# How far apart the rows of one load lie: 48 adjacent rows per partition in place of groups of 8

## The chip, the cores and the metric

The kernel runs on one core of a Trainium2 chip. The metric is device time in microseconds (us), lower is better. "The Trainium skill" names the notes on the chip; its pages are cited by title. A packet is one contiguous piece of a transfer, carried by one of the core's 16 DMA engines; a transfer has landed when its completion is counted. Packet durations, counts and start times, where given, are from the packet records of the trace; everything else is from views of the profile, of which the main lines are shown.

## The reference

```python
x = np.random.randn(8192, 8192).astype(np.float32)      # 256 MiB
return np.linalg.norm(x, ord=np.inf, axis=1)            # max |x| of each row, 8192 results
```

The input is read once, and one number is kept per row of 32 KiB. So this is a stream of loads with a reduction behind it.

## The kernel before

Each partition takes 64 rows: 48 in the bulk, fetched by 24 loads of 8 MiB (two adjacent rows, 64 KiB, per partition), and 16 in a tail, whose pieces get smaller towards the end so that little work is left after the last byte. Three buffers hold tiles. VectorE reduces. SP (SyncE) issues the loads, ACT (ScalarE) issues two of the three outputs.

```python
TAIL = [[8192]]*8 + [[4096,4096]]*5 + [[2048]*4]*2 + [[2048,2048,2048,1024,512,512]]

G = 4; B = 2; BUFS = 3                       # defaults of the function
n_bulk_rows = rows // P - n_tail             # 48
A = n_bulk_rows // (G * B)                   # 6
split = n_bulk_rows * P
x_b   = x[:split].rearrange("(a p n b) c -> a n p (b c)", p=P, a=A, n=G, b=B)
out_b = out[:split].rearrange("(a p n b) -> p a (n b)", p=P, a=A, n=G, b=B)
x_t   = x[split:].rearrange("(p t b) c -> t p (b c)", p=P, b=B)      # tail, pitch 512 KiB
...
for a in range(A):
    for n in range(G):
        t = sbuf.tile([P, B * cols + 16], F32, tag="t")
        nc.sync.dma_start(out=t[:, : B * cols], in_=x_b[a, n])
        absmax(r_bulk[:, a, n * B : (n + 1) * B], t[...])
nc.scalar.dma_start(out=out_b, in_=r_bulk[:])
for i in range(0, n_tail, B):                # the tail, smaller and smaller pieces
    ...
        nc.sync.dma_start(out=t[:, at : at + w], in_=x_t[i // B][:, at : at + w])
        ...
```

With G = 4, a partition holds 8 adjacent rows of each of 6 blocks. Seen from one load, the 128 pieces lie 8 x 32 KiB = 256 KiB apart; this distance is the pitch. The output of the bulk has, per partition, 6 runs of 8 numbers: 768 runs of 32 B.

## Time and profile before

| | before |
|---|---|
| time, median | 629.97 us (3 runs, 629.9 to 630.3) |
| bytes read | 268.44 MB, 427 GB/s over the span |
| one bulk load | 19.34 us, from one reduction's start to the next |
| one bulk reduction | 17.22 us |

Lines from the page of the profile: bytes moved in 40 slices of the span; the group of the bulk reductions (busy us, mean ns, then idle time before them and its cause); and two groups of DMA issues with the time from issue to landing.

```profile
span 628.1 us, 196 instructions
GB/s 401 413 455 413 455 413 455 413 455 413 455 413 455 409 459 413 455 413 455 413 455 413 455 413 455 413 455 413 455 405 430 434 435 432 420 432 432 424 426 274
...
L63 DVE TENSOR_REDUCE r_bulk<-t 128x2 f32<-128x16384 f32 x24 | 413.3, 17219 | 70.5 <-DMA t<-in_x_dram 70.5
...
t<-in_x_dram SPq DMA_DIRECT2D x24, 40.7
out_dram<-r_bulk ACTq DMA_DIRECT2D x1, 24.0 KB, 57.9
```

The reductions need 413 us and wait 70.5 us, always for loads; a load of 8,388,608 B in 19.34 us is 433.7 GB/s. The load stream is the bound. Longer windows (columns: stretch, its length, busy time of VectorE and GpSimd, clock, DMA share, GB/s):

```profile
42.00:484.00 442.00, 395.34 (x23) 0.00 (x0) 1.00 1.00 433
484.00:519.00 35.00, 35.00 (x6) 0.00 (x0) 1.00 1.01 432
519.00:560.00 41.00, 40.62 (x7) 0.00 (x0) 1.00 1.00 429
560.00:604.00 44.00, 43.06 (x12) 0.00 (x0) 1.00 1.00 426
```

First SP's waits (in total, times, longest), then the same wait in the chain that ended last (start us, us, what):

```profile
SPq L82 <- DMA out_dram<-r_bulk: 23.2, 1, 23.2
```

```profile
519.10 0.33 SPq L82
519.43 23.23 another core or an unknown queue
542.67 0.33 SPq L82
```

A tail load is not issued until the bulk's output has landed. The program says why: the DMAs use eight completion counters in turn, and the load eight places after the output needs the output's counter (in the trace both name counter 102). No data is involved.

### The profile page before, as it was taken

To read this page: it belongs to the slowest core of one execution; us is meant where nothing else is said; L and a number is where in the kernel's file an instruction comes from. 1 tells how busy PE (TensorE), PEld (TensorE's weight loads), DVE (VectorE), ACT (ScalarE), POOL (GpSimd) and SP (SyncE) were. 2 spreads that over 40 slices of the span, in tenths; PEclk is the share of its full clock that TensorE was granted. 3 is DMA by queue.
4 is the path that set the end of the run, shared out by engine and by line. 5 is a ranking of instruction groups with operands and counts; after the bars stand their busy time and mean duration, and the time that the engine had idled before them with its cause. 6 is when DMAs were issued, how large, how long until landed. Compare 5 with 4: busy or idle time off the path is not lost.

```text
span 628.1 us, 196 instructions
## 1 busy us (share of the span) xinstructions
DVE 552.7 (88%) x58; POOL 0.2 (0%) x4
## 2 busy tenths in 40 slices
DVE  0588988889988889888898888998889999999998
POOL 0000000000000000000000000000000000000000
DMA  9999999999999999999999999999999999999996
GB/s 401 413 455 413 455 413 455 413 455 413 455 413 455 409 459 413 455 413 455 413 455 413 455 413 455 413 455 413 455 405 430 434 435 432 420 432 432 424 426 274
DMA packets 9138, 268.49 MB, mean 427 GB/s; under 512 B 1968, under 2 KB 1968, under 8 KB 2352
## 3 DMA queue, kind: packets, MB, share of 16 engines
q1 hardware_dynamic: 8208, 268.44, 99.1%
q10 hardware_dynamic: 928, 0.03, 0.1%
q14 instruction: 2, 0.02, 0.0%
HBM read 268.44 MB, written 0.03 MB: 427 GB/s over the span
## 4 chain that ended last, share of the span: by engine, by line
DMA 64%; DVE 30%; another core or an unknown queue 4%; issue 1%; SPq 0%
DMA t<-in_x_dram 64%; DVE r_bulk L63 23%; DVE part L63 5%; DVE t L63 1%; SPq L82 0%; DVE r_fin L63 0%; SPq L68 0%
## 5 line engine op out<-in xcount | busy, mean ns | idle before, releaser
L63 DVE TENSOR_REDUCE r_bulk<-t 128x2 f32<-128x16384 f32 x24 | 413.3, 17219 | 70.5 <-DMA t<-in_x_dram 70.5
L63 DVE TENSOR_REDUCE part<-t 128x1 f32<-128x4096 f32 (+2 forms) x26 | 130.0, 5067 | 1.3 <-DMA t<-in_x_dram 1.3
L63 DVE TENSOR_REDUCE t<-t 128x1 f32<-128x2048 f32 (+2 forms) x5 | 8.6, 1746 | 0.4 <-DMA t<-in_x_dram 0.4
L60 DVE MEMSET part<- 128x60 f32 x1 | 0.1, 108 | 0.8 <-PEq L114 0.8
L63 DVE TENSOR_REDUCE r_fin<-t 128x1 f32<-128x517 f32 x1 | 0.7, 692 | 0.0
L63 DVE TENSOR_REDUCE r_tail<-part 128x15 f32<-128x60 f32 x1 | 0.2, 216 | 0.0
L114 POOL MEMSET const-bfloat16-1.0<- 128x1 bf16 x1 | 0.1, 101 | 0.0
L114 POOL MEMSET const-uint8-127<- 128x1 uint8 x1 | 0.1, 101 | 0.0
L114 POOL MEMSET const-float32-0.0<- 128x1 f32 x1 | 0.1, 98 | 0.2 <-issue 0.2
L114 POOL MEMSET const-float32-1.0<- 128x1 f32 x1 | 0.1, 98 | 0.0
## 6 DMA issues: line engine op xcount, KB each, us to landing
t<-in_x_dram SPq DMA_DIRECT2D x8, 4096.0 KB, 37.0
t<-in_x_dram SPq DMA_DIRECT2D x10, 2048.0 KB, 30.4
t<-in_x_dram SPq DMA_DIRECT2D x11, 1024.0 KB, 24.6
t<-in_x_dram SPq DMA_DIRECT2D x1, 512.0 KB, 15.9
t<-in_x_dram SPq DMA_DIRECT2D x2, 256.0 KB, 13.2
t<-in_x_dram SPq DMA_DIRECT2D x24, 40.7
out_dram<-r_bulk ACTq DMA_DIRECT2D x1, 24.0 KB, 57.9
out_dram<-r_tail ACTq DMA_DIRECT2D x1, 7.5 KB, 5.6
```

The costliest lines, as they stand in the source:

```text
L60: nc.vector.memset(part[:], 0.0)
L63: nc.vector.reduce_max(out=o, in_=i, axis=X, apply_absolute_value=True)
L114: nc = _bacc.Bacc("TRN2", target_bir_lowering=False, num_devices=1)
```

## The change

The intent is a simpler layout: one block, in which a partition holds all its 48 bulk rows side by side, and writes its results as one run of 192 B.

```diff
-    G: int = 4,
+    G: int = 24,
```

A becomes 1. Pieces of one load now lie 48 x 32 KiB = 1.5 MiB apart, and one load touches addresses over 192 MiB in place of 32 MiB. The output of the bulk becomes 128 runs of 192 B. The instructions on the other engines, the sizes and the order of loads are the same.

## The prediction

> **What bounds the kernel now.** The load stream. The table of windows gives 433 GB/s at a DMA share of 1.00 from 42 to 484 us, nearly all of the bulk. One 8 MiB bulk load arrives each 19.34 us (starts of the reductions in the timeline): 433.7 GB/s. The Trainium skill, "DMA: Bandwidth & Descriptors", section Specifications, puts the fabric ceiling at 435 GB/s; the trace agrees, so nothing is left to win in the bulk. VectorE needs 17.22 us per tile and waits about 2.1 us each time; it follows the loads.
>
> **What the change does.** The 24 loads of 128 pieces of 64 KiB stay, in the same order and size; so do the reductions, buffers and tail. Two things change.
>
> 1. Pieces of one load lie 1.5 MiB apart in place of 256 KiB. The skill (same page, Latency and other measured facts, "HBM row pitch at large powers of two") reports copies that lose rate at pitches of 2 MiB (164 GB/s) and 4 MiB (103), with 207 at 512 KiB and 214 when padded, and only infers aliasing. 1.5 MiB is three times 512 KiB: modulo 2, 4, 8 or 16 MiB its pieces fall on the same set of places as those of pitch 512 KiB. The tail of this very kernel has pitch 512 KiB, and there the windows give 432 GB/s (484 to 519 us, and 560 to 574). So I expect no loss: 19.3 us per bulk load as before. If the pitch cost 1% of rate, that would be 4.6 us over the bulk.
>
> 2. The bulk's output is 128 runs of 192 B in place of 768 of 32 B. Now it takes 57.9 us from issue to landing: 48 small packets on each of 16 engines, each apparently taking its turn behind a 32 KiB load packet (estimate: 4 MiB at 433 GB/s is 9.7 us for 8 packets per engine, 1.21 us each; 48 x 1.21 = 58). With 8 per engine it should land in about 10 us. The waits show the SP queue held for 23.2 us by that output, from 519.4 to 542.7 us in the chain, before the next tail loads. This wait should vanish. It is worth little: meanwhile the queue still had loads to run (426 GB/s from 519 to 545 us), and only 543 to 546 us shows a dip, to 371 GB/s: (1 - 371/433) x 3 us = 0.4 us. The page gives that whole queue 0.1% of the DMA time, so the saved packets add at most 0.5 us.
>
> **On the critical path:** 0 for the pitch, -0.3 to -0.8 us for the output.
>
> **Predicted time:** 629.5 us, 80% range 628.4 to 631.2. Chances: faster by over 2%: 0.01; within 2%: 0.95; slower by over 2%: 0.04.
>
> **What would show it.** Right: reductions of the bulk start 19.3 us apart, VectorE idle before them about 70 us again, 433 GB/s in the bulk windows; the bulk's output lands in about 10 us; the 23 us wait is gone from SP's waits and the chain; no dip after 543 us. Wrong on the pitch: bulk loads further apart, GB/s lower at a DMA share still 1.00, VectorE idle longer. Wrong on the output: it still takes over 30 us, or the wait stays, or the wait goes and the total gains over 1 us.
>
> **What would make it wrong.** HBM treating 1.5 MiB worse than the tail's 512 KiB (one load now spans 192 MiB, not 32); earlier tail loads meeting the reductions so that buffers come free at a worse time; the wait on SP resting on something other than that output.

## The result, and the profile after

| | before | after |
|---|---|---|
| time, median of 6 runs each | 630.14 us (629.90 to 630.55) | 630.34 us (629.88 to 630.69) |
| ratio of after to before | | 1.0003, 95% interval 0.9990 to 1.0015 |
| bulk's output, issue to landing | 57.9 us | 14.3 us |
| SP's wait on it | 23.2 us | none |

Ratios here and below are the mean time of one kernel's runs over that of the other's of the same rounds, so not quite the ratio of the medians quoted.

The time is the same. The page, the windows, and the chain where the wait was:

```profile
span 628.6 us, 196 instructions
...
L63 DVE TENSOR_REDUCE r_bulk<-t 128x2 f32<-128x16384 f32 x24 | 413.3, 17220 | 71.0 <-DMA t<-in_x_dram 71.0
...
t<-in_x_dram SPq DMA_DIRECT2D x24, 40.7
out_dram<-r_bulk ACTq DMA_DIRECT2D x1, 24.0 KB, 14.3
```

```profile
42.00:484.00 442.00, 394.87 (x23) 0.00 (x0) 1.00 1.00 433
484.00:519.00 35.00, 35.00 (x5) 0.00 (x0) 1.00 1.00 430
519.00:560.00 41.00, 40.66 (x7) 0.00 (x0) 1.00 1.00 430
560.00:604.00 44.00, 42.97 (x12) 0.00 (x0) 1.00 1.01 427
```

```profile
485.10 51.65 DVE part L63 x6
536.75 0.02 issue
536.77 0.33 SPq L82
```

The wait of 23 us is gone from the chain, and the stretch in which it sat (519 to 560 us) moves 430 GB/s in place of 429. The tail did not get shorter: from the first tail reduction to the end of the span it is 628.1 - 484.62 = 143.5 us before and 628.6 - 485.10 = 143.5 us after.

### The profile page after: what moved, and what is told of

Its sections match the earlier page's. It is cut to its first block, busy times and chain, and to the rows that moved or that the text cites. A ratio compares the mean times of both kernels' runs of the same rounds, so it can differ in the third digit from the quotient of the medians.

```text
span 628.6 us, 196 instructions
## 1 busy us (share of the span) xinstructions
DVE 552.7 (88%) x58; POOL 0.2 (0%) x4
## 4 chain that ended last, share of the span: by engine, by line
DMA 65%; DVE 32%; issue 1%; another core or an unknown queue 0%; SPq 0%
DMA t<-in_x_dram 65%; DVE r_bulk L63 23%; DVE part L63 8%; DVE t L63 1%; DVE r_fin L63 0%; SPq L68 0%; SPq L82 0%
## 6 DMA issues: line engine op xcount, KB each, us to landing
out_dram<-r_bulk ACTq DMA_DIRECT2D x1, 24.0 KB, 14.3
```

## The experiments

Four questions: is the output's form worth anything? Was the 23 us wait hidden, and by how much? Does the pitch matter at all on this chip, and if so, is it distance or a power of two? And does the length of a piece matter? Ten kernels were run. The first call (e1 to e4) ran on one chip, the other two on another; before took the same time on both, to 0.3 us. Seven of the ten put results in wrong places, so that one thing changes at a time; in each of those the loads, reductions and sizes are those of a right kernel.

| run | pitch of the bulk | tail | bulk's output | median us | ratio to before (95%) |
|---|---|---|---|---|---|
| before | 256 KiB | 512 KiB | 32 B runs | 630.04 to 630.33 | 1 |
| after | 1.5 MiB | 512 KiB | 192 B | 630.34 | 1.0003 (0.9990 to 1.0015) |
| e1 | 256 KiB | 512 KiB | 192 B | 629.86 | 0.9997 (0.9984 to 1.0010) |
| e2 | 1.5 MiB | 512 KiB | 32 B | 630.38 | 1.0007 (0.9995 to 1.0019) |
| e3 | 256 KiB | 512 KiB | 8 B | 638.23 | 1.0130 (1.0117 to 1.0143) |
| e5 | 64 KiB | 512 KiB | 192 B | 630.39 | 0.9998 (0.9984 to 1.0012) |
| e10 | 512 KiB | 512 KiB | 192 B | 630.70 | 1.0008 (0.9996 to 1.0021) |
| e9 | 1 MiB | 1 MiB | 192 B | 641.35 | 1.0183 (1.0163 to 1.0203) |
| e8 | 1.94 MiB | 1.94 MiB | 192 B | 629.97 | 0.9995 (0.9983 to 1.0008) |
| e4 | 2 MiB | 2 MiB | 192 B | 662.68 | 1.0524 (1.0496 to 1.0552) |
| e6 | 1.5 MiB, 16 KiB pieces | 512 KiB | 192 B | 634.31 | 1.0066 (1.0049 to 1.0083) |
| e7 | 2 MiB, 16 KiB pieces | 2 MiB | 192 B | 724.14 | 1.1493 (1.1438 to 1.1549) |

### e1 and e2: one half of the change at a time

e1 keeps the loads of before and takes the output's form of after; e2 does the reverse.

```diff
 e1, from before
-    out_b = out[:split].rearrange("(a p n b) -> p a (n b)", p=P, a=A, n=G, b=B)
+    out_b = out[:split].rearrange("(p k) -> p k", p=P)
-    nc.scalar.dma_start(out=out_b, in_=r_bulk[:])
+    nc.scalar.dma_start(out=out_b, in_=r_bulk[:].rearrange("p a k -> p (a k)"))
 e2, from after
-    out_b = out[:split].rearrange("(a p n b) -> p a (n b)", p=P, a=A, n=G, b=B)
+    out_b = out[:split].rearrange("(s p k) -> p s k", p=P, s=6)
-    nc.scalar.dma_start(out=out_b, in_=r_bulk[:])
+    nc.scalar.dma_start(out=out_b, in_=r_bulk[:].rearrange("p a (s k) -> p (a s) k", s=6))
```

> Loads as before (256 KiB apart), output as after (128 runs of 192 B, so results land in wrong places on purpose). Theory H (the wait was hidden: the DMA engines had loads queued through all of it, so the output's form is worth nothing): within 0.3 us of before, about 630.1, with the output landing in about 14 us and SP's wait on it gone. Rival C (cancellation: the output's form gains 0.3 to 0.8 us and the wider pitch loses as much): 629.3 to 629.8, ratio 0.9987 to 0.9995. If the pitch makes the start of the stream late, the third bulk reduction starts at 61.5 us here as in before; if that was chance, anywhere from 61.4 to 62.0.

> Loads as after (1.5 MiB apart), output in 768 runs of 32 B as before (results in wrong places on purpose). Theory H: about 630.2, within 0.3 us of after, although the output takes about 58 us again and holds SP for about 23 us. Rival C: 630.5 to 631.1. If the pitch makes the start late, the third bulk reduction starts at about 61.9 us as in after.

e1 took 629.86 us and e2 630.38 us. The waits followed the output's form and not the pitch: SP's wait on the output is gone in e1, and in e2 it is there again at 23.1 us:

```profile
SPq L84 <- DMA out_dram<-r_bulk: 23.1, 1, 23.1
```

And yet e2 is within 0.1 us of after (630.34, from another call). So adding the 23 us wait back costs nothing that shows (theory H). The large cancellation of theory C is not there either: e1 is 0.2 us below before, less than C asked for, and the interval of its ratio spans 1. A pitch effect of some 0.4 us, from the start of the stream, is hinted at: the third bulk reduction starts at 61.47 us before and 61.34 in e1, at 61.93 in after and 61.67 in e2. It is taken up again with e5 and e10.

### e3: a longer wait

How much longer could the output take before it costs time? e3 splits it into 3072 runs of 8 B.

```diff
 e3, from before
-    out_b = out[:split].rearrange("(a p n b) -> p a (n b)", p=P, a=A, n=G, b=B)
+    out_b = out[:split].rearrange("(s p k) -> p s k", p=P, k=2)
-    nc.scalar.dma_start(out=out_b, in_=r_bulk[:])
+    nc.scalar.dma_start(out=out_b, in_=r_bulk[:].rearrange("p a (s k) -> p (a s) k", k=2))
```

> As before, but the output in 3072 runs of 8 B, 192 per DMA engine (wrong places on purpose), to lengthen the wait on SP. One packet per 1.21 us load packet would make it 232 us. Theory S (the wait limits itself: once the loads already issued, 226 MiB, have run dry at about 548 us, the small packets no longer queue behind loads and finish at once): the wait ends near 549 to 552 us, DMA idles 2 to 4 us, total 632 to 635. Rival L (each small packet keeps its turn time whatever else is queued): SP held until about 717 us, total over 790. If the wait had no margin at all in before, the form of the dose does not matter and the total stays within 0.5 us.

It took 638.23 us, 8.2 us more than before. The wait did limit itself, as theory S said: SP was held 35.4 us and not 200. From the table of windows and the chain of e3:

```profile
545.00:549.00 4.00, 3.45 (x2) 0.00 (x0) 1.00 1.01 426
549.00:552.00 3.00, 3.00 (x1) 0.00 (x0) 1.00 0.52 28
552.00:555.00 3.00, 3.00 (x2) 0.00 (x0) 1.00 0.00 0
555.00:557.00 2.00, 2.00 (x1) 0.00 (x0) 1.00 0.53 106
557.00:558.00 1.00, 1.00 (x1) 0.00 (x0) 1.00 0.84 344
```

```profile
519.63 35.39 another core or an unknown queue
555.02 0.02 issue
555.03 0.33 SPq L84
```

The loads that had been issued ran dry at about 549 us. Of the 3072 small packets 946 had been through at 549.0 us, at the pace of about one per load packet; the other 2126 were through at 551.1 us. The size was off: expected 2 to 4 us of idle DMA and 632 to 635 us in total, measured 6.7 us and 638.23. The 6.7 us run from the start of the last load packet (549.4 us) to the start of the next (556.0 us): 1.7 us for the remaining packets, 3.9 us in which no packet moves until SP sees the output landed (555.0 us), and 1 us to the first new bytes; then the stream needs until 558 us to fill up. Expectation S had left out the landing and the fill.

This also gives an estimate of the margin in before: its SP was free at 542.7 us, and in e3 the loads already issued lasted to about 549 us, so the wait was hidden with some 6 us to spare.

### e4: a pitch of 2 MiB

The whole matrix in one layout, 64 adjacent rows per partition, with a correct result.

```diff
 e4, from after
-    x_b = x[:split].rearrange("(a p n b) c -> a n p (b c)", p=P, a=A, n=G, b=B)
-    x_t = x[split:].rearrange("(p t b) c -> t p (b c)", p=P, b=B)
+    x_p = x.rearrange("(p r b) c -> r p (b c)", p=P, b=B)
 (loads from x_p[a * G + n] and x_p[A * G + i // B]; outputs likewise)
```

> As after, but the whole matrix in one layout: 64 adjacent rows per partition, bulk and tail both at a row pitch of 2 MiB, a power of two; correct result. Theory P0 (with one core loading, the DMA engines bound each packet at 2.42 us per 64 KiB and the pitch does not show): 630.2, bulk reductions 19.34 us apart. Rival P2 (a power-of-two pitch loses rate, in the proportion 164 to 214 that the skill's page gives for copies at 2 MiB): 25 us per bulk load, total about 820. The tail here has pieces of 16 KiB and less at 2 MiB: P2 would show at least there, as packets of 16 KiB over 0.61 us.

It took 662.68 us, 5.2% more than before. P0 is refuted: the pitch shows. P2's total of about 820 us is refuted as well; only its weaker form holds, that packets of 16 KiB take over 0.61 us (0.64 on average here). The profile is of the slowest of the six runs (666.14 us). The windows of e4:

```profile
0.00:60.00 60.00, 28.00 (x3) 0.20 (x4) 1.00 0.97 367
60.00:120.00 60.00, 50.52 (x4) 0.00 (x0) 1.00 1.01 428
200.00:460.00 260.00, 229.69 (x14) 0.00 (x0) 1.00 1.00 432
480.00:520.00 40.00, 40.00 (x4) 0.00 (x0) 1.00 1.01 410
600.00:640.00 40.00, 28.35 (x10) 0.00 (x0) 1.00 1.01 313
```

In all of these stretches the DMA engines are busy; they only move less. The first three reductions start at 26.8, 49.3 and 71.3 us (22.8, 42.1 and 61.5 before); from 200 us on the loads come at full rate from the same kind of addresses; and the tail, whose pieces get shorter, is slow again, down to 313 GB/s. Packets of 8 KiB took 0.49 us on average in place of 0.31. Of the 36.3 us that this profile is longer than that of before, the bulk lost 12.5 (its last reduction starts at 480.00 us, not 467.49), 9.8 of them by the third load; the tail lost the other 23.8. So most of the 5.2% is not from the 64 KiB pieces of the bulk but from the shorter ones of the tail.

### e8 and e9: distance, or a power of two?

1.5 MiB was free and 2 MiB cost 33 us, so either distance matters and 1.5 MiB was just near enough, or the power of two does. e8 goes almost as far as 2 MiB with an odd multiple of 64 KiB; e9 comes nearer, with a power of two.

```diff
 e8, from after (62 adjacent rows; the last pair per partition from the 256 rows left over)
+    x_p = x[: 62 * P].rearrange("(p r b) c -> r p (b c)", p=P, b=B)
+    x_e = x[62 * P :].rearrange("(p b) c -> p (b c)", b=B)
 e9, from after (two blocks of 32 adjacent rows)
+    x_p = x.rearrange("(a p r b) c -> a r p (b c)", a=2, p=P, b=B)
```

> As the 2 MiB run, but 62 adjacent rows per partition: row pitch 1.94 MiB (31 x 64 KiB), and the last pair of rows of each partition taken from the 256 rows left over (results in wrong places on purpose). Theory A (power-of-two alignment: engines that read the same place modulo a large power of two slow one another; distance itself costs nothing): 629.7 to 630.5, like before, and reductions 19.3 us apart from the first. Rival D (distance, or the span of addresses that one load touches: 0 at 256 KiB, about 0.4 us at 1.5 MiB, 32 us at 2 MiB): over 650, with the first four loads 20 to 27 us apart as in the 2 MiB run.

> Row pitch 1 MiB in bulk and tail (two blocks of 32 rows per partition; wrong places on purpose). Theory A: between 512 KiB or 1.5 MiB (under 0.5 us) and 2 MiB (32 us), so 633 to 645, with the loss in the first loads and in the tail. Rival D: like after or less, 629.9 to 630.4, since 1 MiB is less than 1.5 MiB. The two differ in sign against after: A slower by over 2 us, D not slower.

Windows of e8, then of e9:

```profile
0.00:60.00 60.00, 34.55 (x3) 0.20 (x4) 1.00 0.98 419
60.00:120.00 60.00, 52.37 (x4) 0.00 (x0) 1.00 1.01 437
```

```profile
0.00:60.00 60.00, 28.99 (x3) 0.20 (x4) 1.00 0.98 375
60.00:120.00 60.00, 50.80 (x4) 0.00 (x0) 1.00 0.99 426
200.00:460.00 260.00, 228.99 (x14) 0.00 (x0) 1.00 1.00 430
480.00:640.00 160.00, 156.32 (x34) 0.00 (x0) 1.00 0.96 411
```

The tail of before, to compare with the last line of e9:

```profile
468.00:628.00 160.00, 156.00 (x34) 0.00 (x0) 1.00 0.97 414
```

The nearer pitch is the slower one: 1 MiB costs 11.0 us (641.35 against 630.33), 1.94 MiB costs nothing (629.97). Distance, and the span of addresses, is out: of the pitches tried, the two powers of two from 1 MiB up cost time, and no other does. These two are also the only multiples of 1 MiB; whether 3 MiB, say, would cost too was not tried. One part of the expectation for e9 missed: its tail lost nothing. From the last bulk reduction's start to the end of the span it took 160.5 us (479.79 to 640.3), as before (467.49 to 628.1: 160.6). All of its loss, 12.3 us in the profile, is in the bulk, which thus lost as much at 1 MiB as at 2 MiB (12.5); what sets e4's 33 us apart is its tail.

### e10 and e5: 512 KiB and 64 KiB

```diff
-    G: int = 4,
+    G: int = 8,      (e10; e5 has G = 1; both with the 192 B output of e1)
```

> Bulk at 512 KiB (groups of 16 rows), tail unchanged at 512 KiB, output in 192 B runs (wrong places on purpose). The prediction's argument was that 1.5 MiB, three times 512 KiB, meets the same places modulo powers of two as 512 KiB. If so: as after, 630.2 to 630.5, with the third bulk reduction at about 61.7 to 61.9 us. If the 0.4 us of after come from distance: as with 256 KiB, 629.8 to 630.0, third reduction at about 61.4.

> Bulk pitch 64 KiB, so that each load is one contiguous 8 MiB block; output in 192 B runs (wrong places on purpose). Theory A with its floor at the DMA engines' own rate: 629.6 to 630.0, no better than 256 KiB with the same output (629.86), 19.3 us per load. A rival in which narrower is always better would give under 629.3.

e10 took 630.70 us, 0.2 us over the range named, with the third reduction at 61.90 us: like after, as the prediction's argument asked. But e5, where each load is one contiguous block, took 630.39 us where 629.6 to 630.0 was expected, and in its profile the loads between 60 and 100 us came late by 0.5 us in all, much as after had lost 0.5 us before 80 us. So the start-up loss of about 0.4 us that the profiles of after, e2, e10 and e5 show, and those of before, e1 and e8 do not, has no order by pitch; e3, with the loads of before, lost 0.2 us in the same way between 158 and 178 us. In time none of these runs (e3 apart) differs from before by more than its interval. Whether the change costs 0.3 us or nothing stays open; it is not over 1 us.

### e6 and e7: short pieces

```diff
 e6 from after, e7 from e4
-            nc.sync.dma_start(out=t[:, : B * cols], in_=x_b[a, n])
+            for c in range(0, B * cols, 4096):
+                nc.sync.dma_start(out=t[:, c : c + 4096], in_=x_b[a, n][:, c : c + 4096])
 (e7: x_p[a * G + n] in place of x_b[a, n])
```

> As after (1.5 MiB, correct result), but each bulk tile is fetched by 8 loads of 128 pieces of 16 KiB in place of one of 128 pieces of 64 KiB. Control for the next run. Theory A (1.5 MiB is harmless by its odd factor, whatever the piece): as after plus small packet overhead; the tail's own packets (611 ns for 16 KiB, 2418 for 64 KiB) give 1.1% more per byte, so about 635 us. Rival B (only long pieces hide the pitch): packets of 16 KiB well over 0.65 us, total over 650.

> As the 2 MiB run (correct result), with the bulk fetched in pieces of 16 KiB. In the 2 MiB run the loss of the bulk died out after some 100 us. Theory K (short pieces keep the engines in step, or bring them back into step, as in that run's tail, where 8 KiB packets took 0.49 us in place of 0.31): the loss lasts, 16 KiB packets take 0.70 us or more on average, total over 720. Rival F (the loss fades with time whatever the piece): 660 to 675, packets of 16 KiB at 0.61 to 0.63 us on average after the first 100 us.

e6 took 634.31 us, close to the 635 estimated from the tail's packets: at 1.5 MiB short pieces cost their own overhead only (0.613 us per 16 KiB packet on average). e7 took 724.14 us, 14.9% more than before, and its loss does not fade:

```profile
60.00:120.00 60.00, 45.10 (x4) 0.00 (x0) 1.00 1.01 382
200.00:460.00 260.00, 201.49 (x12) 0.00 (x0) 1.00 1.00 380
```

The same window of e6, the control at 1.5 MiB:

```profile
200.00:460.00 260.00, 229.89 (x14) 0.00 (x0) 1.00 1.01 430
```

That the loss lasts is what theory K forecast; the mean packet was 0.686 us, a little under the 0.70 named. Rival F is out: with 64 KiB pieces the rate was back at 432 GB/s in that window, with 16 KiB pieces it stays at 380. (The tail, also at 2 MiB, lost 30.8 of the 97.3 us by which this profile is longer than that of before.) That engines start in step on like addresses, and drift apart when pieces are long, would fit the bulk of e4 and e7. It does not explain why the short pieces of e9's tail lost nothing at 1 MiB, and no run shows which address each engine reads when. So the reason of K is not shown, only that the loss depends on pitch and piece.

## Why the prediction was right

**The bound: right.** Loads at 433 GB/s before and after, a reduction every 19.3 us, VectorE idle 70.5 and 71.0 us. The Trainium skill's fabric ceiling ("DMA: Bandwidth & Descriptors", Specifications, 435 GB/s) agrees with 433.

**No cost from the pitch: right, by an argument of two steps, of which one is borne out and one was lucky.** The first step was that 1.5 MiB, three times 512 KiB, meets the same places modulo powers of two as 512 KiB. The runs agree with it: 512 KiB 630.70 us, 1.5 MiB 630.34, 1.94 MiB 629.97, but 1 MiB 641.35 and 2 MiB 662.68. The second step took the tail, which ran at full rate at 512 KiB, as a sign that the bulk would. That does not hold in general: in e9 the tail ran at full rate at 1 MiB, while the bulk at the same pitch lost 12.3 us. It is e10, and not the tail, that shows the bulk unharmed at 512 KiB. The caution was well placed: the loss that the skill's row on large powers of two reports for copies at 2 MiB is there in plain loads too, if smaller, and a change from 48 to 64 rows would have cost 5.2%.

**The output lands sooner, and the wait goes: right in kind, size a little off.** 14.3 us in place of the 10 predicted. The small packets went out from 488.6 to 497.9 us, about the 9.7 us of the estimate; what it left out is the 3.4 us between issue and the first packet, and 1.6 us from the last packet to the landing. That they take turns with the load packets agrees with the skill (same page, "Queues, rings and completion order"), which says that an engine goes round its queues packet by packet. In before the 768 small packets took from 488.3 to 541.1 us, 48 per engine and so 1.10 us for each, close to the 1.21 us of one load packet. The packets themselves are not slow: they took 9 to 15 ns each.

**The worth of the output, -0.3 to -0.8 us: not borne out.** This is the one term that failed. The step was: "only 543 to 546 us shows a dip, to 371 GB/s: (1 - 371/433) x 3 us = 0.4 us". The dip is no gap. Here are windows of 3 us of before, then of after, where nobody waits for the output:

```profile
537.00:540.00 3.00, 3.00 (x1) 0.00 (x0) 1.00 0.97 415
540.00:543.00 3.00, 3.00 (x1) 0.00 (x0) 1.00 1.04 448
543.00:546.00 3.00, 2.62 (x2) 0.00 (x0) 1.00 0.87 371
```

```profile
534.00:537.00 3.00, 3.00 (x2) 0.00 (x0) 1.00 0.94 404
537.00:540.00 3.00, 3.00 (x1) 0.00 (x0) 1.00 1.06 459
543.00:546.00 3.00, 2.66 (x2) 0.00 (x0) 1.00 0.93 399
```

The view books each packet of 0.6 to 1.2 us in the window where it starts, so windows of 3 us swing by tens of GB/s in both kernels. Clipped to each microsecond, the packets of before fill the engines to between 1.00 and 1.01 in every microsecond from 536 to 552 us. The wait of 23 us was hidden entirely, and removing it is worth nothing that shows. e2 shows the same from the other side: the wait back in, and no time added. The upper bound for the saved packets, 0.5 us, was not used up either: the tails of the two profiles have the same length to 0.1 us.

**The total:** 630.34 us against 629.5 predicted, within the range of 628.4 to 631.2; the difference is mostly that term, and the change made no difference clear of noise. The range was wide enough for "no change" and for the predicted gain alike, so the hit on the total says nothing for the output's term.

## What to carry to other kernels

When a load stream is at its ceiling, check the row pitch against large powers of two: here 512 KiB, 1.5 and 1.94 MiB were free, while 1 MiB cost 1.8% and 2 MiB 5.2%, or 14.9% with the bulk in 16 KiB pieces. Check the stage that you change, and not another at the same pitch: short pieces were harmed at 2 MiB and not at 1 MiB, long ones at both. A wait in the issuing queue, even one that the chain of waits names, costs nothing while the queue holds issued loads; ask when they run dry (here some 6 us after the wait ended), and test it by lengthening the wait. Do not read a gap from windows only a few packets long.

## What the Trainium skill lacked or had wrong

- "DMA: Bandwidth & Descriptors", Latency and other measured facts, "HBM row pitch at large powers of two": it has copies of 16 KiB pieces only. Plain loads lose less, and the loss depends on the piece: at 2 MiB the bulk in 64 KiB pieces lost 12.5 us in all (367 GB/s in the first 60 us, 432 from 200 us on), while in 16 KiB pieces the loss lasted (380 GB/s, against 430 at 1.5 MiB), as compared with 164 of 214 GB/s in the page.
- The same row says nothing of 1 MiB, which cost 1.8%, or of pitches such as 1.5 MiB (630.34 us) and 1.94 MiB (629.97 us), which cost nothing measurable; the only pitches off a power of two in it are 4 MiB with a padding of 4 KiB or of 192 B. Its loss at 512 KiB (207 of 214) was not seen in loads: ratio 1.0008, interval 0.9996 to 1.0021.
- The same page, "Queues, rings and completion order", tells of arbitration by packet but not of the consequence: an output of many short runs is slowed by the number of its runs while loads are queued. 48 runs per engine took 57.9 us to land, 8 took 14.3; in e3, once the loads had run dry, the last 2126 runs went through in about 2 us.
- No page that was read says that reuse of a completion counter can hold a load for an unrelated output; here it was 23.2 us, hidden.
